# A batched matmul with scale and add: a five-transfer head, four weight rows per partition, stride-two transposes, one more transposed pair on VectorE

## The chip, the cores and the metric

The kernel runs on one core of one Trainium2 chip. The metric is the device time of one execution in microseconds (us); lower is better. A core has five engines that run side by side: TensorE (PE in the profile, with its weight loads as PEld), VectorE (DVE), ScalarE (ACT), GpSimd (POOL) and SyncE (SP), which here only issues transfers. The transfers themselves run on 16 transfer engines between device memory (HBM) and on-chip memory (SBUF).

## The reference

```python
batch, m, k, n = 16, 512, 1024, 768      # all float32
out = (scale * np.matmul(x, weight) + add_value).astype(np.float32)
```

x is 33.6 MB, the weight 3.1 MB, the addend 25.2 MB, the output 25.2 MB: 87.03 MB to move in one execution, whatever the order.

## The kernel before

The 8192 rows of x are cut into 64 tiles of 128. Each x tile is cast to bf16, its bf16 values are taken two by two as 4-byte words, and the words are transposed, most tiles by TensorE with the identity (four 128x128 transposes a tile, copied out by ScalarE), some in pairs of tiles by VectorE in 32x32 blocks. Then come 16 matmuls a tile: eight slices of the contraction, each on 512 and on 256 columns. VectorE adds the scaled result to the addend in place, and the sum is stored. All transfers are issued in one order, STREAM: x, weight (w), addend (a), outputs (o; l and r are the left 512 and right 256 columns of the last tile), each with first tile and count.

```python
STREAM = [
    ("x", 0, 3), ("w", 0, 2), ("w", 2, 2), ("w", 4, 2), ("x", 3, 1), ("w", 6, 2),
    ("a", 0, 3), ("x", 4, 4), ("a", 3, 1), ("x", 8, 4), ("a", 4, 4), ("x", 12, 4),
    ("a", 8, 8), ("x", 16, 8), ("a", 16, 8), ("x", 24, 8), ("a", 24, 8), ("o", 0, 8),
    # ... cut ...
    ("o", 40, 8), ("o", 48, 8), ("o", 56, 4), ("o", 60, 1), ("o", 61, 1), ("o", 62, 1),
    ("l", 63, 1), ("r", 63, 1),
]
PAIRS = [14, 19, 24, 29, 34, 39, 44, 49, 54]          # first tiles of the pairs that VectorE transposes
# ... cut ...
w_v = weight.rearrange("(c p r) n -> p c r n", p=P, r=2)   # two neighbouring rows a partition

def transpose(t, pieces=1):                            # on TensorE
    # ... cut ...
    pairs = xb_tiles.pop(t).bitcast(fp32)
    # ... cut ...
    for c in range(KC):
        nc.tensor.transpose(tp[:, c, :], pairs[:, c * P:(c + 1) * P], identity)
    # ... cut: ScalarE copies tp to xt, even and odd rows apart ...

def turn_pair(t0, a):                                  # on VectorE
    # ... cut: vt is allocated, pairs is the 4-byte view of the two cast tiles ...
    for b in range(0, P, 32):
        nc.vector.transpose(
            vt[b:b + 32, :, 32 * a:32 * a + 32], pairs[32 * a:32 * a + 32, :, b:b + 32])

def product(t, j, cols):
    # ... cut: a PSUM buffer is taken ...
    for n0, n1 in cols:                                # (0, 512) and (512, 768)
        nc.tensor.matmul(mm_tiles[t, cols[0]][:, n0:n1], lhs(t, j), w_bf[:, j, n0:n1],
                         start=(j == 0), stop=(j == KJ - 1))
```

The x tiles share 16 slots in SBUF, the addend and the outputs share 32, and three buffers in PSUM, the memory that TensorE writes, take the products. SyncE can have eight transfers outstanding; each further one waits for an earlier one.

## Time and profile before

| | before |
|---|---|
| time, median of 6 runs | 210.82 us (210.56 to 210.93) |
| profiled span | 209.2 us |
| TensorE busy / end of its last matmul | 94% / 203.6 us |
| transfers: bytes, share of 16 engines | 87.03 MB, 97.7% |
| last store: issued, landed | 204.06, 208.2 us |
| VectorE, GpSimd, ScalarE busy | 63%, 30%, 24% |

The lines that carry the prediction stand in it. Four others are needed to read the profile. The first is the TensorE clock in 40 slices of 5.2 us, in tenths of full speed; the others are groups of instructions: line, engine, operation, count, busy us and mean ns of one.

```profile
PEclk9889979999999999999999999999999999999997
L120 DVE STREAM_TRANSPOSE vt<-vx 32x256 f32<-32x256 f32 x144 | 62.7, 435 | 6.2 <-POOL vx L109 4.0
L146 PE MATMUL tp<-identity,xb 128*128 128x128 f32 x184 | 28.3, 277 | 5.4 <-POOL xb L136 3.0
L146 PEld LDWEIGHTS tp<-identity,xb 128*128 128x128 f32 x184 | 21.7, 143 | 12.1 <-POOL xb L136 3.4
```

The clock dips to 7 tenths in the sixth slice, just after TensorE has waited 3 us for x. The two transposes, on VectorE and on TensorE, are the instructions that the change makes read at stride two, that is, every second 4-byte word.

### The profile page before, as it was taken

How to read it: one execution, taken by the hardware profiler on the slowest of the kernel's cores; microseconds unless marked ns; L12 is line 12 of the kernel's file. 1: busy time of each engine (PE TensorE's matmuls, PEld its weight loads, DVE VectorE, ACT ScalarE, POOL GpSimd, SP SyncE). 2: the span in 40 equal slices, each digit the busy share in tenths (PEclk: the TensorE clock that was granted, in tenths of full speed). 3: DMA queues.
4: the chain of work that ended last, by engine and by line, in shares of the span. 5: the costliest groups of instructions: out<-in, count | busy, mean ns of one | idle time of the engine just before them, and what ended most of it. 6: DMA issues, size and time to landing. Idle time of an engine off the chain costs nothing.

```text
span 209.2 us, 2988 instructions
## 1 busy us (share of the span) xinstructions
PE 196.4 (94%) x1218; PEld 119.5 (57%) x1218; DVE 131.1 (63%) x223; ACT 49.3 (24%) x52; POOL 63.2 (30%) x69
## 2 busy tenths in 40 slices
PE   7599499999999999999999999999999999999990
PEld 2355256656665666566665666565666656666550
DVE  0545413309969969898697886949994994223340
ACT  2513113233103112113032031121130230332310
POOL 1310536420292090503903606303503039100000
PEclk9889979999999999999999999999999999999997
DMA  6999999999999999999999999999999999999993
GB/s 233 418 431 447 423 408 441 451 445 407 404 481 410 418 432 418 432 451 415 437 417 436 436 421 425 442 434 423 423 432 445 445 409 418 432 447 426 409 402 152
DMA packets 5485, 87.21 MB, mean 417 GB/s; under 512 B 608, under 2 KB 736, under 8 KB 2016
## 3 DMA queue, kind: packets, MB, share of 16 engines
q1 hardware_dynamic: 5472, 87.03, 97.7%
q8 instruction: 9, 0.15, 0.3%
q14 instruction: 4, 0.03, 0.0%
HBM read 61.87 MB, written 25.17 MB: 416 GB/s over the span
## 4 chain that ended last, share of the span: by engine, by line
PE 90%; DMA 3%; DVE 2%; ACT 1%; POOL 0%; issue 0%; ACTq 0%; POOLq 0%
PE mm L168 80%; PE tp L146 10%; DMA xs<-in_x_dram 3%; DVE ao L235 1%; ACT xt L152 1%; DVE ao L204 1%; POOL xb L136 0%; DVE xb L132 0%; DVE ao L176 0%; ACTq L152 0%; POOLq L136 0%
## 5 line engine op out<-in xcount | busy, mean ns | idle before, releaser
L168 PE MATMUL mm<-w_bf,xt 128*128 128x512 bf16 (+1 forms) x736 | 130.8, 331 | 0.6 <-DVE ao L204 0.4
L168 PEld LDWEIGHTS <-xt 128*128 128x128 bf16 x736 | 69.6, 99 | 50.8 <-ACT xt L152 11.4
L176 DVE SCALAR_TENSOR_TENSOR ao<-mm,ao 128x768 f32<-128x768 f32 (+2 forms) x62 | 58.3, 944 | 54.1 <-PE mm L168 35.3
L152 ACT COPY xt<-tp 128x1024 bf16<-128x1024 bf16 (+1 forms) x49 | 46.6, 961 | 146.0 <-PE tp L146 146.0
L120 DVE STREAM_TRANSPOSE vt<-vx 32x256 f32<-32x256 f32 x144 | 62.7, 435 | 6.2 <-POOL vx L109 4.0
L136 POOL CAST xb<-xs 128x1024 bf16<-128x1024 f32 x43 | 43.2, 1040 | 56.2 <-DMA xs<-in_x_dram 46.5
L168 PE MATMUL mm<-w_bf,vt 128*128 128x512 bf16 (+1 forms) x288 | 49.7, 326 | 0.0
L168 PEld LDWEIGHTS <-vt 128*128 128x128 bf16 x288 | 28.2, 98 | 17.5
L109 POOL CAST vx<-xs 128x1024 bf16<-128x1024 f32 x18 | 18.3, 1040 | 53.8 <-DVE vt L120 44.7
L146 PE MATMUL tp<-identity,xb 128*128 128x128 f32 x184 | 28.3, 277 | 5.4 <-POOL xb L136 3.0
L146 PEld LDWEIGHTS tp<-identity,xb 128*128 128x128 f32 x184 | 21.7, 143 | 12.1 <-POOL xb L136 3.4
L104 DVE CAST w_bf<-ao 128x768 bf16<-128x768 f32 x8 | 4.1, 557 | 3.8 <-DMA ao<-in_weight_dram 3.8
L132 DVE CAST xb<-xs 128x512 bf16<-128x512 f32 x3 | 1.9, 696 | 5.6 <-DMA xs<-in_x_dram 5.6
L94 PE MATMUL warm<-zeros 128*128 128x512 bf16 x10 | 4.3, 617 | 1.2 <-DVE zeros L82 1.2
L134 POOL CAST xb<-xs 128x512 bf16<-128x512 f32 x2 | 1.6, 834 | 5.5 <-DMA xs<-in_x_dram 5.5
L94 PEld LDWEIGHTS <-zeros 128*128 128x128 bf16 x10 | 1.3, 140 | 3.4 <-issue 2.2
L204 DVE TENSOR_SCALAR ao<-mm 128x768 f32<-128x768 f32 x2 | 1.8, 952 | 2.3 <-PE mm L168 2.3
L235 DVE TENSOR_TENSOR ao<-ao 128x768 f32<-128x768 f32 x3 | 2.7, 950 | 0.0
L134 ACT CAST xb<-xs 128x512 bf16<-128x512 f32 x1 | 0.6, 618 | 4.8 <-DMA xs<-in_x_dram 4.8
L134 ACT ACT_TABLE_LOAD x1 | 1.3, 1283 | 0.7 <-PEq L279 0.7
L201 ACT ACTIVATE ao<-mm 128x768 f32<-128x768 f32 x1 | 0.8, 817 | 0.0
L82 DVE MEMSET zeros<- 128x256 uint32 x1 | 0.3, 272 | 0.9 <-PEq L279 0.9
(6 smaller groups left out, 0.9 us busy)
## 6 DMA issues: line engine op xcount, KB each, us to landing
xs<-in_x_dram SPq DMA_DIRECT2D x6, 4096.0 KB, 27.3
ao<-in_add_value_dram SPq DMA_DIRECT2D x7, 3072.0 KB, 24.3
out_dram<-ao SPq DMA_DIRECT2D x7, 3072.0 KB, 31.2
xs<-in_x_dram SPq DMA_DIRECT2D x3, 2048.0 KB, 22.0
ao<-in_weight_dram SPq DMA_DIRECT2D x4, 768.0 KB, 9.5
xs<-in_x_dram SPq DMA_DIRECT2D x1, 1536.0 KB, 6.0
ao<-in_add_value_dram SPq DMA_DIRECT2D x1, 1536.0 KB, 23.7
out_dram<-ao SPq DMA_DIRECT2D x1, 1536.0 KB, 11.7
```

The lines of the kernel that those rows point to most:

```text
L94: nc.tensor.matmul(warm[:, 0:CUT], zeros[:, 0:P], zeros, start=True, stop=True)
L104: nc.vector.tensor_copy(w_bf[:, j + i, :], ao[:, s + i, :])
L109: nc.gpsimd.tensor_copy(vx[:, i, :], xs[:, (t0 + i) % X_SLOTS, :])
L120: nc.vector.transpose(vt[b:b + 32, :, 32 * a:32 * a + 32], pairs[32 * a:32 * a + 32, :, b:b + 32])
L134: other(xb[:, K // 2:K], src[:, K // 2:K])
L136: nc.gpsimd.tensor_copy(xb, src)
L146: nc.tensor.transpose(tp[:, c, :], pairs[:, c * P:(c + 1) * P], identity)
L152: nc.scalar.copy(dst[:, c:c + q, :, :], src[:, c:c + q, :, :])
L168: nc.tensor.matmul(mm_tiles[t, cols[0]][:, n0:n1], lhs(t, j), w_bf[:, j, n0:n1], start=(j == 0), stop=(j == KJ - 1))
L176: nc.vector.scalar_tensor_tensor(a, mm_tiles[t, part][:, n0:n1], float(scale), a, op0=mybir.AluOpType.mult, op1=mybir.AluOpType.add)
L204: nc.vector.tensor_scalar(ao[:, EARLY_AT + t, :], mm_tiles[t, BOTH[0]][:, 0:N], float(scale), None, op0=mybir.AluOpType.mult)
L235: nc.vector.tensor_add(ao[:, t, :], ao[:, EARLY_AT + t, :], ao[:, t, :])
```

## The change

Its intent is a shorter list of larger transfers, above all at the start, and less work on TensorE. The weight is laid out so that a partition holds four neighbouring rows and one load brings 12 KB in one run to each; the 4-byte words of x must then be taken at stride two, so that they meet the same rows. One pair more goes to VectorE, and the later transfers are reordered.

```diff
 STREAM = [
-    ("x", 0, 3), ("w", 0, 2), ("w", 2, 2), ("w", 4, 2), ("x", 3, 1), ("w", 6, 2),
-    ("a", 0, 3), ("x", 4, 4), ("a", 3, 1), ("x", 8, 4), ("a", 4, 4), ("x", 12, 4),
-    ("a", 8, 8), ("x", 16, 8), ("a", 16, 8), ("x", 24, 8), ("a", 24, 8), ("o", 0, 8),
-    ... cut ...
+    ("x", 0, 4), ("w", 0, 4), ("w", 4, 4), ("a", 0, 4), ("x", 4, 4), ("x", 8, 4),
+    ("a", 4, 4), ("x", 12, 4), ("a", 8, 8), ("x", 16, 8), ("a", 16, 8), ("x", 24, 8),
+    ("o", 0, 8), ("a", 24, 8), ("x", 32, 8), ("a", 32, 8), ("x", 40, 8), ("o", 8, 8),
+    ("o", 16, 8), ("a", 40, 8), ("x", 48, 8), ("a", 48, 8), ("x", 56, 8), ("o", 24, 8),
+    ("o", 32, 8), ("a", 56, 8), ("o", 40, 8), ("o", 48, 8), ("o", 56, 4), ("o", 60, 2),
+    ("o", 62, 1), ("l", 63, 1), ("r", 63, 1),
 ]
-PAIRS = [14, 19, 24, 29, 34, 39, 44, 49, 54]
+PAIRS = [14, 19, 24, 29, 34, 39, 44, 49, 54, 59]
-    w_v = weight.rearrange("(c p r) n -> p c r n", p=P, r=2)
+    w_v = weight.rearrange("(h p q) n -> p h (q n)", p=P, q=4)
     # turn_pair
-        pairs = vx_tiles[t0].bitcast(fp32).rearrange("p i (c k) -> p (i c) k", k=P)
+        pairs = vx_tiles[t0].bitcast(fp32).rearrange("p i (h k c) -> p (i h) c k", k=P, c=2)
     # transpose
-            nc.tensor.transpose(tp[:, c, :], pairs[:, c * P:(c + 1) * P], identity)
+            nc.tensor.transpose(tp[:, c, :], pairs[:, c // 2, c % 2, :], identity)
     # ... cut: the weight load takes four rows, the head starts with four x tiles ...
```

## The prediction

> **What bounds the kernel now.** I read the busy slices first, then the transfer queue, then the chain of waits, then the last transfers one by one. The slices and the queue:
>
> ```profile
> PE   7599499999999999999999999999999999999990
> DVE  0545413309969969898697886949994994223340
> DMA  6999999999999999999999999999999999999993
> q1 hardware_dynamic: 5472, 87.03, 97.7%
> PE 90%; DMA 3%; DVE 2%; ACT 1%; POOL 0%; issue 0%; ACTq 0%; POOLq 0%
> 24.40:203.60 179.20, 179.00 (x1136) 110.26 (x1136) 120.07 (x205) 42.50 (x42) 58.75 (x59) 0.99 1.00 429
> ```
>
> The reader is to see that two things are full at once. The chain (fifth line) gives 90% to TensorE. But the transfers are busy in every slice but the first and last, for 97.7% of the span, and in the stretch from 24.4 to 203.6 us (last line: length, busy PE, PEld, DVE, ACT, POOL, clock, DMA share, GB/s) their share is 1.00 at 429 GB/s. Which of them sets the end is read at the end itself, where the last stores are issued (start, length) and land (size, us from issue to landing):
>
> ```profile
> 192.75 0.33 SPq L262 DMA_DIRECT2D out_dram<-ao  x1
> 195.82 0.33 SPq L262 DMA_DIRECT2D out_dram<-ao  x1
> 198.89 0.33 SPq L262 DMA_DIRECT2D out_dram<-ao  x1
> 201.96 0.33 SPq L262 DMA_DIRECT2D out_dram<-ao  x1
> 203.45 0.33 SPq L262 DMA_DIRECT2D out_dram<-ao  x1
> 204.06 0.33 SPq L262 DMA_DIRECT2D out_dram<-ao  x1
> ```
>
> ```profile
> out_dram<-ao SPq DMA_DIRECT2D x1, 1536.0 KB, 11.7
> out_dram<-ao SPq DMA_DIRECT2D x1, 384.0 KB, 9.6
> out_dram<-ao SPq DMA_DIRECT2D x1, 384.0 KB, 7.4
> out_dram<-ao SPq DMA_DIRECT2D x1, 384.0 KB, 5.3
> out_dram<-ao SPq DMA_DIRECT2D x1, 256.0 KB, 4.4
> out_dram<-ao SPq DMA_DIRECT2D x1, 128.0 KB, 4.1
> ```
>
> Issue plus time to landing: the store of tiles 56 to 59 lands at 192.75 + 11.7 = 204.45, then tiles 60, 61, 62 at 205.4, 206.3, 207.3, then the two pieces of tile 63 at 207.85 and 208.2. They land one behind another, a 384 KB store every 0.95 us, although tiles 60 and 61 were issued over 6 us earlier: the store queue has a backlog when TensorE stops at 203.6. The first load of the kernel shows what an empty queue costs: 1536 KB issued at 0.74 landed at 6.75, of which 1.573 MB / 418 GB/s = 3.76 us is data, so about 2.25 us is fixed. The last store, 128 KB, would alone take some 2.25 + 0.3 = 2.55 us; it took 4.1. So I put the transfers as the bound of the end, by about 1.5 us over TensorE, in spite of the chain. The whole is then 3.0 us of start, 87.03 MB at 429 GB/s = 202.9 us, and a tail of some 2 to 3 us.
>
> **What the Trainium skill says.** "DMA: Bandwidth & Descriptors", section "Where 436 GB/s comes from", gives 435 GB/s as the ceiling of the SBUF side; 429 here agrees with a queue at its limit. Its section "Why small descriptors are slow (HBM only)" charges each packet a small fixed overhead; this trace agrees in kind: the weight loads with 6 KB per partition landed 1.89 us apart, 416 GB/s. "SBUF — State Buffer", section "Door 1: The DMA port swizzle", says lines are 16 bytes and that two hits per line keep full bandwidth; a pair at stride two (4 of every 8 bytes) just does that. No instruction of the kernel before reads SBUF in that way, so the trace can't confirm it. "Vector Engine (DVE) Microarchitecture Reference", section 3.8, says the 32x32 transpose sustains one element per cycle per lane; 256 elements in 435 ns fit that with a fixed part.
>
> **The change part by part.**
>
> (1) Head. Before, x0-2, three weight pairs, x3, the last weight pair: 5.24 MB, the last weight at 3.16 + 12.4 = 15.5 us. After, x0-3, then two loads of four weight rows per partition: the same 5.24 MB, so the last weight also lands near 15.5. But the first x lands with 2.10 MB in place of 1.57: 6.75 + 0.524/0.418 = 8.0 us, and the first weights at 8.0 + 1.573/0.418 = 11.8 instead of 8.6. Half of the weights now come at once at 15.5; their four casts take 4 x 0.52 us on VectorE and their products 24 matmuls, about 4 us, so the three early tiles end near 20.6 instead of 19.5. That is hidden, because TensorE then waits for x4-7 anyhow (3.04 us idle before 24.36). x4-7 now comes behind four tiles of the addend instead of three: +0.393 MB, +0.9 us. TensorE's steady run starts near 25.2 instead of 24.36: **+0.85 us on TensorE**, none on the transfers, which stay fed.
>
> (2) One more pair, tiles 59 and 60. Eight PE transposes go; the chain gives four as 0.44 us: **-0.88 us on TensorE**. Added are 16 vector transposes of 435 ns = 7.0 us of VectorE at 170 to 190 us, where its slices are 2 to 4 tenths full. Hidden. (1) and (2) cancel on TensorE, which ends near 203.6 as before.
>
> (3) Stride-two reads. All 176 PE transposes and 160 vector transposes that remain now read their pairs at stride two: no instruction more per tile; I take their durations as unchanged, so 0.
>
> (4) Transfers. 33 in place of 38, same 87.03 MB. Each small one costs above its bytes: a weight pair 1.89 us against 0.786 MB / 431 GB/s = 1.825, x3 1.28 against 1.22, a 384 KB store 0.95 against 0.91, so 0.04 to 0.06 each. Five fewer: 5 x 0.05 = **-0.25 us on the queue**.
>
> (5) Order of the stream. I replayed the queue first in, first out, at 9.73 us for eight x tiles and 7.3 us for eight addend or output tiles (the landings before fit: 73.1, 80.5, 87.8, 97.5, 104.7, 114.4 us). At no point does the queue run dry, so the total stays. What moves is who comes late. The addend of 24-31 lands at 87.8 instead of 80.5, about when tile 24 ends. x48-55 waits behind the store of 8-15 and lands near 146.1 instead of 131.4. GpSimd then casts tile 48 and the pair 49, 50 by 149.2, VectorE needs 4 x 1.78 + 3 x 0.96 us after that, and is done at 159.3; TensorE reaches tile 49 at about 159.4 plus its delay of 0.85. The addend of 56-63 lands near 185 instead of 177.8; tile 56 ends at 182.6, three PSUM buffers cover it. All three are tight and just hidden.
>
> Sum: the queue -0.25, TensorE about 0 and not the bound by 1.5 us. 210.84 - 0.25 = **210.6 us**.
>
> **The rivals.** (a) *TensorE is the bound*, as the chain says. Then (1) and (2) still cancel, and a late x48 adds directly: 211 to 213. For it: 90% of the chain. Against: the last stores are spaced by bytes and not by TensorE's 3.07 us per tile. (b) *The restart clock*. In the 3.04 us wait before 24.36 the clock fell, and the next 16 matmuls took 4.28 us instead of 2.63. If the new wait is shorter, TensorE gains 1.65 us; for the queue as the bound this buys nothing. (c) *Stride two is slow*. If vector transposes took 267 ns more each (256 elements at a second cycle), a cycle of five tiles would need 5 x 0.96 + 16 x 0.70 = 16 us of VectorE where TensorE needs 3 x 3.07 + 2 x 2.63 = 14.5: about +1.5 us for each of ten pairs, 220 or more. If PE transposes doubled, some 40 tiles times 0.44 us: 220 to 228. For it: nothing here was ever read so. Against: two hits per line. (d) *x48 later than the replay by 2 us or more*: TensorE stalls by as much less its 1.5 us of slack: 211 to 213.
>
> **Range and chances.** The centre is 210.6. Below, only the queue can give, at most another 0.7 us if larger packets in the head run faster than I count: 209.8. Above, one or two of the tight hand-overs failing by 1 to 2 us: 212.2. Faster by over 2% (below 206.6) would need more than 435 GB/s or fewer bytes: 0.03. Slower (above 215.1) needs stride two to cost, or a stall of several us: 0.09. Within 2%: 0.88.
>
> **What would show it.** Right: transfer share still 1.00 near 430 GB/s after 24 us; the last stores again landing about 0.9 us per 384 KB, and later than TensorE's end by over 3.5 us; the vector transposes still 435 ns, four PE transposes still 0.44 us; x4-7 near 24.1 us; x48-55 landing near 146. Wrong: vector transposes near 700 ns with VectorE at nines all through, PE transposes longer, TensorE waits in the middle over 2 us in sum, a slice with the transfers under 9, or a last store landing in 2.6 us, which would say that TensorE set the end.

## The result, and the profile after

The changed kernel took 211.17 us (median of 6 runs, 211.05 to 211.5) against 210.82 us before. The ratio is 1.0021, with a 95% interval of 1.0008 to 1.0034. Ratios in this document are the mean time of one kernel's runs over that of the other's of the same rounds, so not quite the ratio of the medians quoted. Executions over 1.5% slower than the fastest of the same kernel are left out of the means. The change is thus within 2%, as predicted, and inside the range of 209.8 to 212.2; but the small gain of 0.25 us that the prediction put at its centre is a small loss of about 0.4 us.

First the page of the changed kernel, with the same groups as above (their lines are now L117 and L144), and the same stretch from 24.4 to 203.6 us (length, then busy us with instruction counts of PE, PEld, DVE, ACT, POOL, the clock, the transfers' share and GB/s).

```profile
PEclk9859999999999999999999999999999999999997
DMA  6999999999999999999999999999999999999993
q1 hardware_dynamic: 4752, 87.03, 97.4%
L117 DVE STREAM_TRANSPOSE vt<-vx 32x256 f32<-32x256 f32 x160 | 69.7, 436 | 10.3 <-POOL vx L106 7.9
L144 PE MATMUL tp<-identity,xb 128*128 128x128 f32 x176 | 29.3, 292 | 4.4 <-DVE xb L130 3.0
L144 PEld LDWEIGHTS tp<-identity,xb 128*128 128x128 f32 x176 | 24.8, 206 | 10.9 <-issue 3.9
24.40:203.60 179.20, 177.88 (x1128) 110.40 (x1128) 130.74 (x224) 40.48 (x40) 61.30 (x60) 1.00 1.00 429
```

Nothing of the bound has moved: the transfers still have share 1.00 at 429 GB/s. Packets fell from 5472 to 4752. The vector transposes cost what they did, 436 ns against 435. The TensorE transposes do not: the weight-load record of one went from 143 to 206 ns. And the dip of the clock in the sixth slice is gone. The first steady tile, its four transposes and then its 16 matmuls, shows it, as the chain of waits has it (before, then changed: start, length, both in us):

```profile
24.36 0.66 PE tp L146 x4
25.01 4.28 PE mm L168 x16
```

```profile
25.56 0.74 PE tp L144 x4
26.30 2.64 PE mm L166 x16
```

Three of the last stores of the changed kernel (tiles 60 and 61, tile 62, the right part of tile 63), issue (start, length) and, in the second block, time to landing:

```profile
199.11 0.33 SPq L260 DMA_DIRECT2D out_dram<-ao  x1
202.22 0.33 SPq L260 DMA_DIRECT2D out_dram<-ao  x1
204.32 0.33 SPq L260 DMA_DIRECT2D out_dram<-ao  x1
```

```profile
out_dram<-ao SPq DMA_DIRECT2D x1, 768.0 KB, 7.8
out_dram<-ao SPq DMA_DIRECT2D x1, 384.0 KB, 5.6
out_dram<-ao SPq DMA_DIRECT2D x1, 128.0 KB, 4.4
```

They land at 206.9, 207.8 and 208.7 us: again 0.9 us per 384 KB, again long after TensorE's last matmul, which ends at 203.8 us. Before, the last one landed at 208.2.

Why is the end later, with fewer transfers of the same bytes? The packed trace also holds, in records that the views do not print, the moment at which each of the 16 transfer engines completed its part of every transfer. A transfer has landed when the last one has. Taken as the mean over the 16 engines, the changed kernel does gain at first: the first 8.9 MB are done at 23.82 us against 24.05, and at 62 us the lead is still 0.24 us. By 98 us, at the same number of bytes, it is gone (96.29 against 96.26), and it stays gone (near 201 us, 198.84 against 198.81). At the last store the slowest engine is 0.54 us later than before, in these two profiles (the changed kernel's is of a run of 211.48 us, 0.3 us above its median). The distance between the first and the last engine is the key to what follows:

| time between first and last engine, us | before | changed |
|---|---|---|
| transfers that land before 25 us | 0.3 to 0.4 | 0.4 to 0.5 |
| first one after 30 us | 1.82 | 1.82 |
| near 98 us (x of 32 to 39) | 1.86 | 2.61 |
| near 185 us | 2.15 | 2.60 |
| near 201 us (outputs of 48 to 55) | 3.45 | 4.07 |

The two large steps, by 1.3 to 1.5 us each, come right after a transfer that is not the kernel's own. The queue called "instruction" holds nine of them in both kernels, 16 KB each and about 1.05 us on one engine: TensorE's program arrives in pieces while it runs. The first begins near 28 us (29 after the change), the ninth at 190 us before and 188 us after. The others make other engines late: before, one engine is over 1.7 us behind the first at 46 us, two at 56, three at 73 and four at 97, as many as instruction transfers had begun by then. Only the ninth moves the last engine much again (2.15 to 3.46 us), so it came on one that was already late. The rise near 70 us in the changed kernel is taken up below.

### The profile page after: what moved, and what is told of

The parts are those of the page before. It is cut to its first block, busy times and chain, and to the rows that moved or that the text cites. A ratio compares the mean times of both kernels' runs of the same rounds, so it can differ in the third digit from the quotient of the medians.

```text
span 209.7 us, 2975 instructions
## 1 busy us (share of the span) xinstructions
PE 197.1 (94%) x1210; PEld 120.3 (57%) x1210; DVE 139.9 (67%) x239; ACT 47.2 (23%) x50; POOL 65.1 (31%) x69
## 4 chain that ended last, share of the span: by engine, by line
PE 84%; issue 7%; DMA 3%; POOL 2%; ACT 0%; DVE 0%; POOLq 0%; ACTq 0%
PE mm L166 75%; PE tp L144 9%; DMA xs<-in_x_dram 3%; POOL xb L134 1%; POOL xb L132 1%; ACT xt L150 0%; DVE ao L174 0%; POOLq L134 0%; ACTq L150 0%
## 5 line engine op out<-in xcount | busy, mean ns | idle before, releaser
L166 PE MATMUL mm<-w_bf,xt 128*128 128x512 bf16 (+1 forms) x704 | 124.3, 330 | 1.1 <-DVE w_bf L101 0.6
L166 PEld LDWEIGHTS <-xt 128*128 128x128 bf16 x704 | 66.5, 99 | 49.4 <-ACT xt L150 10.9
L150 ACT COPY xt<-tp 128x1024 bf16<-128x1024 bf16 (+1 forms) x47 | 44.6, 959 | 147.0 <-PE tp L144 147.0
L117 DVE STREAM_TRANSPOSE vt<-vx 32x256 f32<-32x256 f32 x160 | 69.7, 436 | 10.3 <-POOL vx L106 7.9
L166 PE MATMUL mm<-w_bf,vt 128*128 128x512 bf16 x320 | 55.3, 326 | 0.0
L166 PEld LDWEIGHTS <-vt 128*128 128x128 bf16 x320 | 31.4, 98 | 19.6 <-DVE vt L117 0.2
L106 POOL CAST vx<-xs 128x1024 bf16<-128x1024 f32 x20 | 20.3, 1040 | 48.3 <-DVE vt L117 38.0
L144 PE MATMUL tp<-identity,xb 128*128 128x128 f32 x176 | 29.3, 292 | 4.4 <-DVE xb L130 3.0
L144 PEld LDWEIGHTS tp<-identity,xb 128*128 128x128 f32 x176 | 24.8, 206 | 10.9 <-issue 3.9
L233 DVE TENSOR_TENSOR ao<-ao 128x768 f32<-128x768 f32 x3 | 4.4, 1509 | 0.0
```

Source lines behind the costliest of these rows:

```text
L106: nc.gpsimd.tensor_copy(vx[:, i, :], xs[:, (t0 + i) % X_SLOTS, :])
L117: nc.vector.transpose(vt[b:b + 32, :, :, 32 * a:32 * a + 32], pairs[32 * a:32 * a + 32, :, :, b:b + 32])
L144: nc.tensor.transpose(tp[:, c, :], pairs[:, c // 2, c % 2, :], identity)
L150: nc.scalar.copy(dst[:, c:c + q, :, :], src[:, c:c + q, :, :])
L233: nc.vector.tensor_add(ao[:, t, :], ao[:, EARLY_AT + t, :], ao[:, t, :])
```

## The experiments

**Theory 1**: the transfers set the end, and TensorE has some 2 us to spare. **Theory 2**, the rival: TensorE sets the end, as the chain of waits says. Under theory 1 a second question: does the mean rate of the transfers count (1b), or the slowest engine, which the instruction transfers make late (1a)?

### Less work on TensorE

```diff
+    def last_j(t):
+        return 6 if t >= 40 else KJ - 1
     def product(t, j, cols):
+        if j > last_j(t):
+            return
 # ... cut: stop=(j == last_j(t)) ...
```

> The changed kernel, but tiles 40 to 63 leave out the last of their eight contraction slices (wrong result on purpose): 24 x 0.33 us = 7.9 us less TensorE work after about 134 us, same transfers. Theory 1 (the transfers set the end, TensorE has 1.5 to 2 us to spare): the time stays within 0.5 us of the changed kernel, 210.7 to 211.4 us. Theory 2 (TensorE sets the end): 5 to 8 us less, near 204.

Measured: 211.47 us (4 runs), ratio to before 1.0027, interval 1.0003 to 1.0051. TensorE's last matmul ended at 202 us and its busy time from 134 to 203.6 us fell from 69.4 to 63.5 us, and nothing came of it. The time is 0.07 us above the band that theory 1 gave and far above that of theory 2. The chain of waits of this run no longer shows TensorE at 84%, as in the changed kernel, but

```profile
PE 52%; DMA 29%; issue 7%; POOL 4%; DVE 3%; ACT 1%; SPq 0%; POOLq 0%; ACTq 0%; DVEq 0%
```

with the stores in it. The chain names the work that was released last; with two limits within 2 us of each other, it may name either.

### Fewer bytes, and both cuts together

```diff
-            nc.sync.dma_start(xs[:, k:k + n, :], rows(x_v, s, n))
+            n_in = 4 if s == 56 else n
+            nc.sync.dma_start(xs[:, k:k + n_in, :], rows(x_v, s, n_in))
```

> The changed kernel, but the last x load brings only tiles 56 to 59; tiles 60 to 63 reuse old rows (wrong result on purpose): 2.1 MB = 4.9 us less on the queue, same TensorE work. Theory 1: the end moves forward until TensorE binds, by 1.5 to 2.2 us: 209.0 to 209.7 us. Theory 2: within 0.3 us of the changed kernel.

> Both cuts together. Theory 1: with TensorE out of the way the queue shows its whole 4.9 us: 206.0 to 206.7 us, although each cut alone gives 2 us or less. Theory 2: the same as the kernel with the TensorE cut alone.

Measured: 209.18 us (5 runs, ratio 0.9907) for the byte cut alone, 206.74 us (4 runs, ratio 0.9803) for both. So 4.9 us of bytes give 2.0 us alone, because TensorE then becomes the limit: it ends at 205.4 us in the profiled run, and the last store finds the queue nearly empty (the timeline, then the list of transfers, whose last column is us from issue to landing):

```profile
205.42 0.42 DVE L174 SCALAR_TENSOR_TENSOR ao<-mm,ao 128x256 f32<-128x256 f32 x1 [0.18 <-PE mm L166]
```

```profile
out_dram<-ao SPq DMA_DIRECT2D x1, 128.0 KB, 1.8
```

The store lands 1.8 us after issue instead of 4.4. The profile is of the slowest of the five runs (210.41 us; the others took 208.87 to 209.22): in it the clock granted from 24.4 to 28.7 us was 0.65, as before the change (0.66), where the profile of the changed kernel has 1.00. So the size of the gain is taken from the median, not from this profile. The cut on TensorE, worth nothing alone, is worth another 2.4 us here. Theory 2 is out; both limits are real and lie about 2 us apart, the transfers in front.

### Fewer instruction transfers

```diff
-        return 6 if t >= 40 else KJ - 1
+        return 5 if t >= 40 else KJ - 1      # second of the two runs: 4
```

> As the first of these, but tiles 40 to 63 leave out two slices: 192 instructions fewer on TensorE, so that the ninth 16 KB instruction transfer, which began at 188 us and after which one of the 16 transfer engines completes 4.1 us behind the first instead of 2.6, should not occur. Theory 1a (the slowest transfer engine sets the end, and instruction transfers make it slow): 8 instruction transfers, last store 1.0 to 1.5 us earlier than in the first of these runs, 209.4 to 210.2 us. Theory 1b (the mean rate of the transfers sets the end): the same as the first of these within 0.3 us. Theory 2: 14 us less than the changed kernel.

Measured: 211.42 us (4 runs, ratio 1.0018). This run missed its aim: the ninth instruction transfer still came, at 200 us, and the distance between the first and last engine still rose from 2.57 to 4.05 us. So the count was lowered further.

> As the run with two slices left out, but three slices (288 TensorE instructions fewer in all, wrong result on purpose), since with 192 fewer the ninth instruction transfer still came, at 200.15 us. Theory 1a (slowest transfer engine sets the end, made late by instruction transfers): 8 instruction transfers, the last stores complete with about 2.6 us between the first and last engine and not 4, and the time is 1.0 to 1.5 us below the runs with one or two slices left out: 209.8 to 210.4 us. Theory 1b (mean rate): 211.2 to 211.5 us as those.

Measured: 209.94 us (4 runs, 209.92 to 209.95), ratio to before 0.9960, interval 0.9946 to 0.9973. Eight instruction transfers, and the last stores complete within 2.46 us from first to last engine. The tail of the transfers shows it directly. The next fences give, for 203 to 210 us in 40 slices of 0.175 us, what the engines moved; first with two slices of the contraction left out (nine instruction transfers), then with three (eight).

```profile
GB/s 456 375 538 328 386 416 416 293 404 304 363 199 269 252 275 193 240 176 94 35 64 18 35 18 23 23 35 18 23 18 0 0 0 0 0 0 0 0 0 0
```

```profile
GB/s 439 456 369 421 427 398 328 398 380 334 287 281 252 246 240 269 187 141 88 53 41 23 0 0 0 0 0 0 0 0 0 0 0 0 0 0 0 0 0 0
```

All 16 engines together move some 430 GB/s, so one moves about 27. In the first fence the row falls to 18 to 35 GB/s with the 22nd slice and stays there for nine slices, 1.6 us: one engine is finishing its share alone. In the second that stretch is missing. TensorE is out of the way in both, as the run with one slice left out showed. Between these two profiles the mean completion of the last store over the 16 engines moved by 0.10 us (206.12 to 206.02), that of the last engine by 1.39 (208.59 to 207.20). Theory 1a holds: the end is the end of the slowest engine, and the ninth instruction transfer costs 1.2 us of it by the two ratios, 1.5 by the medians (the two runs were made on different chips, so the ratios count more). The changed kernel as it is shows the same stretch:

```profile
GB/s 369 527 386 404 421 299 351 211 298 351 439 386 357 410 345 269 158 181 140 94 94 82 47 35 18 23 23 35 18 23 18 0 0 0 0 0 0 0 0 0
```

(same time and slices).

### The pair, the layout, the stream

Three kernels undo one part or do one part alone; the layout alone keeps the old stream and reads two of a partition's four rows per load.

```diff
 # no last pair                       # stream alone: as changed, but
-PAIRS = [14, ..., 54, 59]            -    w_v = ... "(h p q) n -> p h (q n)", q=4
+PAIRS = [14, ..., 54]                +    w_v = ... "(c p r) n -> p c r n", r=2   and stride one
```

> The changed kernel without the added pair 59, 60: TensorE gets its eight transposes back, 2 x 0.48 = 0.96 us more, same transfers. Theory 1 (transfers set the end): within 0.3 us of the changed kernel, 210.9 to 211.5 us. Theory 2 (TensorE): 212.1 us.

> The kernel before with the four-row weight layout and the stride-two reads alone (its own stream and its own nine pairs): 46 tiles times 0.04 us = 1.8 us more on TensorE, transfers as before. Theory 1: TensorE had 1.6 us to spare, so 0 to 0.4 us slower than before: 210.8 to 211.2 us. Theory 2: 1.8 us slower, 212.6 us.

> The changed kernel with the old two-row layout and stride one: its two weight loads then bring two runs of 6 KB per partition each. TensorE gets 44 x 0.04 = 1.8 us back. If the 0.4 us that the change lost come from the stream and its order, this stays at 211.0 to 211.4 us; if they come from the stride-two reads, it falls to 210.4 to 210.8 us.

Measured: 211.35 us without the pair (5 runs, ratio 1.0025), 210.89 us for the layout alone (5 runs, ratio 1.0005, interval 0.9992 to 1.0017), 210.96 us for the stream alone (5 runs, 210.60 to 211.38, ratio 1.0009, interval 0.9995 to 1.0023). The pair's 0.96 us of TensorE is hidden, as theory 1 said. The layout alone is the best look at TensorE's slack: with the same clock dip as before, its stride-two reads delay the end of TensorE's work by 1.8 us, from 203.6 to 205.4, and the time stays. It also separates the cost of the reads: the weight-load record of a transpose takes 206 ns here and 146 with the stream alone. In the run of the layout alone the timeline and the list of transfers end with

```profile
205.43 0.42 DVE L177 SCALAR_TENSOR_TENSOR ao<-mm,ao 128x256 f32<-128x256 f32 x1 [0.18 <-PE mm L169]
```

```profile
out_dram<-ao SPq DMA_DIRECT2D x1, 128.0 KB, 2.4
```

The store that took 4.1 us behind a backlog takes 2.4: the slack of the kernel before was spent, not exceeded. The stream alone is inconclusive on time (its runs scatter by 0.8 us), but its engines lie 2.59 us apart near 98 us, like those of the changed kernel; those of the layout alone 1.77, like before. So in these profiles the extra 0.7 us or so between the engines goes with the stream, not with stride two.

### Which part of the stream

```diff
 # exchange back                      # new head only: old stream after the head
-    ("o", 0, 8), ("a", 24, 8),       # old head only: new stream after the head
+    ("a", 24, 8), ("o", 0, 8),
```

> The changed kernel with one exchange in the stream: the addend of 24 to 31 again ahead of the first output store, as before. In the five transfers that follow 60 us the completion records of the kernels with the changed stream show 2.2 to 2.7 us between the first and last engine, those with the old stream 1.5 to 1.9. Theory 1c (the first store right behind an x load costs the late engines some 0.4 us, for good): spread back to 1.8 us, time 0.4 us less, 210.7 to 210.9. If the order of these two does not matter: 211.1 to 211.4 us and a spread above 2.2 us.

Measured: 211.17 us (6 runs, ratio 1.0016), engines 2.4 us apart near 98 us. That first idea of mine fell: the order of these two does not matter.

> The four-row layout, the new five-transfer head, and from then on the order, the stores and the nine pairs of the kernel before (34 transfers in all). What is open is the 0.2 to 0.4 us by which the changed kernel is slower than before, seen as 0.5 to 0.8 us more between the first and last engine in what completes after 70 us. If the head brings it: a spread above 2.2 us there and 211.0 to 211.4 us. If the later order or the merged stores bring it: a spread of 1.9 us and 210.6 to 210.9 us.

> The opposite: the changed kernel with the old head (thirteen transfers up to the x load of 12 to 15) and all else as changed. If the head brings the loss: a spread of 1.9 us after 70 us and 210.6 to 210.9 us. If the later order does: above 2.2 us and 211.0 to 211.4 us.

Measured: 211.00 us with the new head only (6 runs, ratio 1.0011, interval 0.9998 to 1.0024; 2.56 us near 98 us), 210.79 us with the old head only (5 runs, 210.72 to 210.86, ratio 1.0000, interval 0.9987 to 1.0012; 1.86 us). In the three profiles with the old head (before, layout alone, this one) the engines lie 1.8 to 1.9 us apart near 98 us and 3.3 to 3.5 after the ninth instruction transfer; in those with the new head and nine instruction transfers, 2.2 to 2.6 and 3.6 to 4.1, with one exception. The run of the next section has the new head and, up to its last stores, the changed stream, and yet 2.0 and 3.4 us: the head does not always bring the extra distance. On time the two intervals overlap, but all six runs with the new head (210.87 to 211.33 us) lie above all five with the old one (210.72 to 210.86) of the same rounds, by 0.27 us in the mean. The two kernels differ in the later order and in the last pair too, so a cost of the head of 0.2 to 0.3 us is likely, not shown. What costs it stays open: the engines' extra distance appears between 63 and 81 us, long after the head is over, in the stretch where its lead is lost.

### Which engine is late

```diff
-            nc.sync.dma_start(rows(out_v, s, n)[:, :, n0:n1], ao[:, k:k + n, n0:n1])
+            edges = {56: [0, 104, 128], 60: [0, 120, 128], 62: [0, 88, 128]}.get(s, [0, P])
+            for p0, p1 in zip(edges, edges[1:]):
+                nc.sync.dma_start(rows(out_v, s, n)[p0:p1, :, n0:n1], ao[p0:p1, k:k + n, n0:n1])
```

> A measurement: the last stores are cut by partitions so that they run on fewer engines: tiles 56 to 59 as 104 and 24 partitions, tiles 60 and 61 as 120 and 8, tile 62 as 88 and 40. If the number of engines is the largest number up to 16 that divides the partitions[...], these run on 13, 12, 15, 8, 11 and 10 engines. Theory 1a says one engine is 1.5 us behind all others after the ninth instruction transfer; the pieces that complete late tell in which part of the 16 it lies. If it is engine 8 or above, giving the last stores to the others can win 1 us or more; if it is among 0 to 7, no such cut helps.

Measured: 214.71 us (one run, state unknown), and as many engines completed as expected: 13, 12, 15, 8, 11 and 10. In the piece on eight engines the last one completed 1.3 us behind the next, so the latest engine is among those eight; which of the 16 they are, no run shows. Cutting the stores this way did not win anything in this one run. No correct version was found that beats the kernel before; the old head with the rest of the change equals it (ratio 1.0000).

## Why the prediction was right

**The bound.** "I put the transfers as the bound of the end, by about 1.5 us over TensorE, in spite of the chain" was right. The slack is about 2 us: 1.8 us more on TensorE changed nothing, and 4.9 us less on the queue gave 2.0.

**(1) Head.** The first x was put at 8.0 us and landed at 8.0; the first weights 11.8, landed 11.7; the last 15.5, landed 15.4; x4-7 24.1, landed 24.0. What TensorE made of it was less exact. The early tiles ended at 22.5 us, not 20.6; the clock granted up to 24.4 us was 0.86 against 0.93 before, but no run isolates this. The steady run began at 25.56, not 25.2, as the cast of tile 4 on GpSimd took 1.44 us instead of 1.02. It ran beside VectorE's three additions of two SBUF tiles, of which two took 1.79 us instead of 0.95; before, they were over when the casts began. All of it was hidden.

**(2) The pair.** Right: a pair takes 0.88 us off TensorE at the old price and 0.96 at the new, its vector transposes are hidden, and undoing it let TensorE end at 204.7 us instead of 203.8 and moved the time from 211.17 to 211.35, within the scatter.

**(3) Stride two.** "I take their durations as unchanged, so 0" failed for TensorE. Four transposes took 0.48 instead of 0.44 us in the chain, over 40 tiles of the steady run 1.5 us. For VectorE it held. **Rival (b)**, named and left out of the sum, came true in the profiled run: TensorE waited 1.17 us instead of 3.04, the clock stayed up, and the next 16 matmuls took 2.64 us instead of 4.28. That the shorter wait is the reason isn't shown: with the old head and the rest of the change TensorE waited 2.91 us and the clock from 24.4 to 28.7 us was still 1.00; with fewer bytes it also waited 2.91 us, and the clock was 0.65. So in this profile TensorE's sum is +1.20 for the start, -1.64 for the clock, +1.5 for the stride and -0.88 for the pair, together +0.2; its last matmul ended 0.26 us later. The "about 0" was right by two errors that cancel, which was luck; with the slack found, either alone would have been hidden too.

**(4) Transfers.** The step that failed is "**-0.25 us on the queue**". A saving is there at first, 0.23 us at 24 us on the mean of the engines, but by 98 us it is gone, and a queue over 16 engines ends with its slowest: that one ended 0.54 us later in the profiled runs. The prediction treated the queue as one line with one rate. It had no term for the distance between the engines, which was 3.45 us near the end of the kernel before. Its price of a store was also high: by the completion records one 384 KB store followed another by 0.92 us, not 0.95, against 0.91 for its bytes. That the time still fell into the range is because both terms are tenths of a us, not because the queue was understood.

**(5) Order.** The replay was good to 0.7 us: the addend of 24-31 landed at 88.4 us (predicted 87.8), x48-55 at 146.6 (146.1), the addend of 56-63 at 185.4 (185). All three were hidden, with single TensorE waits of 0.2 us.

The Trainium skill, "Runtime: NRT & Kernel Launch", section "Instruction fetch mechanics", says that an engine's program is refilled in 16 KiB blocks by the sequencer's own queue, and that the cost of crossing a block is "mostly hidden". The block size agrees with the trace. TensorE shows no wait for a block, but the transfers were held up, and with them as the bound the last block cost 1.2 to 1.5 us.

## What to carry to other kernels

When the transfers are full from start to end, look at the last stores one by one: their spacing tells whether bytes or the compute engine set the end, where the chain of waits may name either. If it is the bytes, a cut on the compute engine is worth nothing; and a queue is as late as its slowest engine, so ask what else runs on that engine, the program's own instructions included. Test such a tie with both cuts alone and together.

## What the Trainium skill lacked or had wrong

- "Runtime: NRT & Kernel Launch", section "Instruction fetch mechanics", calls the cost of a 16 KiB block mostly hidden. That leaves out the transfers: when they were saturated, the first and the ninth block put one of the 16 transfer engines 1.3 to 1.5 us behind, and it stayed behind; without the ninth the time fell from 211.42 to 209.94 us.
- No page has a figure for how far apart the 16 engines can complete the same transfer near the end of a kernel with full transfers (before 3.45, changed 4.07 us), or says that instruction blocks set them apart.
- "SBUF — State Buffer", section "Door 1: The DMA port swizzle", gives two hits per 16-byte line as free. That fits VectorE's transposes (435 to 436 ns) but not TensorE's: stride two with 4-byte words, so two hits per line, took the weight-load record from 143 to 206 ns and four transposes from 0.44 to 0.48 us.
